# Casting one product's weights earlier in a convolution's out-projection, and two tiles that change places in the first feed-forward layer

## Chip, cores, metric

The kernel runs as one program on one core of a Trainium2 chip. The metric is device microseconds of an execution; less is better. The median of three runs before the change is 1311.68 us.

## The reference

The model is a trunk of two layers over 512 tokens of width 1024. Each layer has a token mixer and a SwiGLU feed-forward network, every sub-layer with normalisation before and after and with shift, scale and gate from a conditioning vector. Layer 0 mixes with a gated short convolution, layer 1 with a state-space scan. What matters here is the end of the first mixer and the start of the first feed-forward layer:

```python
def short_conv_mixer(h, w_in, conv_w, w_out):
    b_gate, c_gate, v = jnp.split(h @ w_in, 3, axis=-1)
    u = causal_depthwise_conv(c_gate * v, conv_w)
    return (b_gate * u) @ w_out
...
def swiglu_ffn(h, w_in, w_out):
    gate, up = jnp.split(h @ w_in, 2, axis=-1)
    return (jax.nn.silu(gate) * up) @ w_out
...
        y = short_conv_mixer(h, a_w_in[j], a_conv_w[j], a_w_out[j])
        x = x + gate * rmsnorm(y, norm_g[i, 1])
        h = rmsnorm(x, norm_g[i, 2]) * (1.0 + scale) + shift
        y = swiglu_ffn(h, f_w_in[i], f_w_out[i])
```

## The kernel before, in words

**Precision.** All large products are made of float32 values that are split in two: ScalarE casts the value to a rounded high part, VectorE subtracts the high part from the value to get the low part, and TensorE runs three matmuls (high by high, high by low, low by high). So each operand of TensorE has a cast on ACT and a subtraction on DVE behind it, and each weight tile (`whl`, a pool of four buffers) is free again when the last matmul that reads it is done.

**Order.** PE, ACT, DVE and SP each run their instructions in the order in which the source writes them; there is no planner in the two places that change. An instruction that waits holds up everything behind it on its engine.

**The out-projection of the convolution** (L1172 to L1288). Half of its inner dimension is computed with seven block products in place of eight. The table `PRODUCTS` names for each product the PSUM accumulator (A to D), the block of weights (`b11` to `b22`, or a sum that was made in place) and the block of activations. `product(i)` (L1137) is 12 matmuls of 128x512: two blocks of tokens, two blocks of the inner dimension, three parts each. `w_prep(i)` (L1120) casts the two weight blocks of product i on ACT (L1124) and subtracts on DVE (L1125). The products run in the order 1, 2, 0, 3, 4, 5, 6, with some plain matmuls (L408) between the later ones. Product 4 adds to accumulator A, which product 0 used before it, so A is first copied out to `part` (L1252, ACT). Ahead of product 3 the source has:

```python
            product(0)
            pa, pd, less = [tile4([P, 2, T], F32, "part") for _ in range(3)]
            for t in range(2):
                act.copy(pa[:, t, :], bank("A", t))
            lead, todo = ffn_lead(0, tile4), [[] for _ in range(5)]
            w_prep(4)
            product(3)
```

The `gate_b` of L1243 (L1095 on DVE, then the cast L1096 on ACT) makes the last block of gated activations; it stands between product 2 and product 0. The weights of product 4 are block `b22`, which is final once two accumulating DMAs of POOL (L610) have landed.

**The first feed-forward layer** starts while its first six column blocks are still being finished: `rest(i)` (L566) is 18 matmuls of 128x256 that complete block i, and they run in the order 0, 2, 1, 3, 4, 5. Their weights are the tiles `whl4`, which lie in a pool of 22 buffers of 4 KB per partition. Beside them DVE makes sums of the activations h: `vs.value(j)` (L742) adds the two parts of h again, j = 0 to 3 into the tile `va`, j = 4 to 7 into the tile `raw1`; `vs.sums`, `vs.hi` and `vs.lo` (L763, L764, L748, L753, L755) make the split sums `tq` out of them. SP fetches the first weights: `fetch(u)` (L627) loads two halves of a column block into `sg` (the tile `sums_w`, L632 and L633), adds them with an accumulating DMA of POOL (L640, shown in the profile as L1389) and loads another block into `wsu` (L635 to L638). Then come 12 units of seven products each (class `Units`, `product` with its matmuls on L693, 12 of 128x256). For the first unit the order on PE is P1, P5, P2, P6, P3, then P1 of the second unit, then P7 of the first. P6 and P7 use accumulator A again, and each waits until ACT has copied it out (`keep`, L703). On ACT the second `keep` of a unit stands behind the cast of the next unit's `sg` (`split_y`, L646), and that waits for DVE's `sum_y` (L672).

**Memory.** When the convolution's pool of 22 buffers is closed, the feed-forward layer's tiles are laid over the same bytes, in the order of their allocation. The first write into such a tile waits for the last access to each old buffer that lies under it, and for nothing else (`reuse_waits="tile"`). The second pool there is, in order: `tq1` (16 KB), `sums_w` (8 KB), `s1t`, `raw3`, `raw2`, `raw1`, `raw0` (8 KB each). `s1t` holds sums for the second half of the layer; its first write comes after the first units have begun.

Of the kernel before, what the change touches and what calls it, by code (L numbers as in the profile page):

```python
# [8 lines left out]
F32 = mybir.dt.float32  # L9
F32R = mybir.dt.float32r  # L10
# [6 lines left out]
P = 128  # L17
T = 512
# [13 lines left out]
MUL, ADD, SUB = ALU.mult, ALU.add, ALU.subtract  # L32
NS = 16
PRODUCTS = (("A", "b11", "a11"), ("B", "b21", "a12"), ("C", "b22", "a12"), ("D", "b12", "s1"),
            ("A", "b22", "a11"), ("A", "b11", "a21"), ("A", "b21", "a22"))
# [3 lines left out]
def trunk_kernel(  # L39
# [9 lines left out]
    act, dve, pe, pool = nc.scalar, nc.vector, nc.tensor, nc.gpsimd  # L49

    consts = ctx.enter_context(tc.tile_pool(name="consts", bufs=1))
    ps = ctx.enter_context(tc.tile_pool(name="ps", bufs=4, space=PSUM))
# [4 lines left out]
    whl_p = ctx.enter_context(tc.tile_pool(name="whl", bufs=4))  # L57
# [554 lines left out]
    class Units:  # L612
# [73 lines left out]
        def product(self, u, q):  # L686
            kind, k0, r = self.FACTORS[q]
            if q in self.FIRST:
                self.banks[r, u] = (aux_ps if r == "B" else mm_ps)(f"s{r}")
            dst, w = self.banks[r, u][:, HALVES[0]], self.wts[kind, u]  # L690
            for k in range(4):
                for i, (wl, al) in enumerate(((0, 0), (0, 1), (1, 0))):
                    pe.matmul(dst, w[:, wl, k0 + k, :], self.moving(q, k, al), skip_group_check=True,  # L693
                              start=q in self.FIRST and k == 0 and i == 0, stop=k == 3 and i == 2)
# [96 lines left out]
    with ExitStack() as ph:  # L791
# [14 lines left out]
        def tile4(shape, dtype, name):  # L806
            return actp.tile(shape, dtype, tag="a", name=name)
# [84 lines left out]
        def ffn_lead(i, tile4):  # L892
            w1 = f_w_in[i]
            return [lambda later=None, c0=c0: load_lead([(w1, c0, 256)], tile4, later) for c0 in (0, DFF, 256)]
# [7 lines left out]
        with tc.manual_schedule(engines={PE_ENGINE, mybir.EngineType.SP, mybir.EngineType.Activation,  # L902
# [183 lines left out]
            def gate_b(j, psb):  # L1086
                u = us[j]
                if j < 4:
                    if j % 2 == 0:
                        raw_c.append(tile4([P, 2, T], F32, "bur"))  # L1090
                    dve.tensor_mul(raw_c[j // 2][:, j % 2, :], psb, u)
                    acts.append(None)
                    return lambda: None
                a = act_tile(f"bu{j}")
                dve.tensor_mul(u, psb, u)  # L1095
                act.copy(a[:, 0, :], u)  # L1096
                acts.append(a)
                return lambda: dve.tensor_tensor(a[:, 1, :], u, a[:, 0, :].bitcast(F32), SUB)

            raw_c, rows_c, s1_c, w_c, a_c = [], [], [], {}, {}  # L1100
# [6 lines left out]
            def b_(name, p):  # L1107
                c = int(name[2]) - 1
                return rows_c[2 * p + int(name[1]) - 1][:, c * T:(c + 1) * T]

            def a_(name, p):
                if name == "s1":
                    return s1_c[0][:, p, :]
                return raw_c[p][:, int(name[2]) - 1, HALVES[int(name[1]) - 1]]

            def row_sums(dst, x, y, op):
                for p in range(2):
                    dve.tensor_tensor(a_(dst, p), a_(x, p), a_(y, p), op)

            def w_prep(i):  # L1120
                w = w_c[i] = whl_p.tile([P, 2, 2, T], F32R, tag="whl", name="whlo")
                for p in range(2):
                    src = b_(PRODUCTS[i][1], p)
                    act.copy(w[:, 0, p, :], src)  # L1124
                    dve.tensor_tensor(w[:, 1, p, :], src, w[:, 0, p, :].bitcast(F32), SUB)  # L1125
# [36 lines left out]
            def square_begin():  # L1162
                w_prep(2)
                for p in range(2):
                    add_(b_("b22", p), b_("b12", p))

            row45, st_c = [], []
            early = {7: begin_sums, 8: lambda: row_sums("a21", "a11", "a21", SUB), 9: lambda: a_prep(1),
                     10: lambda: a_prep(3), 11: lambda: a_prep(0), 12: sums_end, 13: lambda: a_prep(2),
                     14: lambda: (a_prep(4), a_prep(5)), 15: lambda: (w_prep(1), a_prep(6)), 16: lambda: (square_begin(), row_split()), 17: lambda: w_prep(0)}  # L1170

            for name in OPENING.split():  # L1172
# [18 lines left out]
            for k in range(18):  # L1191
                i, jp = k % 6, 2 + k // 6 * 2
# [42 lines left out]
            early[17]()  # L1235
            product(1)
            w_prep(3)
            product(2)
            row5, src5 = tile4([P, 2, T], F32R, "whl4"), st_c[0][:, 1, :]
            act.copy(row5[:, 0, :], src5)  # L1240
            next(fins[2])
            next(fins[2])
            lows.append(gate_b(KD - 1, tiles[17]))  # L1243
            dve.tensor_tensor(row5[:, 1, :], src5, row5[:, 0, :].bitcast(F32), SUB)
            row45.append((5, row5.rearrange("p i (k f) -> p i k f", k=1), 0))
            for p in range(2):
                add_(b_("b21", p), b_("b22", p))
# [3 lines left out]
            for t in range(2):  # L1251
                act.copy(pa[:, t, :], bank("A", t))  # L1252
            lead, todo = ffn_lead(0, tile4), [[] for _ in range(5)]
            w_prep(4)
            product(3)
            for t in range(2):
                act.copy(pd[:, t, :], bank("D", t))
# [37 lines left out]
        sa = st_p.enter_context(tc.tile_pool(name="sa", bufs=1, reuse_waits="tile"))  # L1295
# [2 lines left out]
        s_first.append(ffp.tile([P, 2, 4, P], F32R, tag="ffy", name="wss"))  # L1298
        tq.insert(0, sa.tile([P, 2, 2, 4, 256], F32R, tag="wxa", name="tq1"))
        sums_w = sa.tile([P, 2, 2, 4, P], F32, tag="wxb", name="sg")  # L1300
        s1t = sa.tile([P, NS // 2, 256], F32, tag="s1t", name="s1t")
        raw = [sa.tile([P, 4, T], F32, tag=f"raw{q}", name=f"raw{q}") for q in (3, 2, 1, 0)][::-1]
        wx, ff4 = [], []

        def s_tile(u):
# [189 lines left out]
        with tc.manual_schedule(engines={PE_ENGINE, mybir.EngineType.SP, mybir.EngineType.Activation,  # L1495
# [153 lines left out]
            for k in range(k0, last + 1):  # L1649
# [10 lines left out]
                q, j = divmod(k - 3, 4)  # L1660
# [42 lines left out]
            for q, item in enumerate(seq):  # L1703
                if item[0] == "s":
                    product(item)
                else:
                    w = w_of[item]
# [753 lines left out]
    with ExitStack() as ph:  # L2461
# [8 lines left out]
        raw = fb.tile([P, NF, T], F32, tag="raw", name="raw")  # L2470
# [418 lines left out]
```

## Time and profile before

| what | value |
|---|---|
| median of 3 runs | 1311.68 us (1311.48 to 1312.21) |
| the profiled execution's own time | 1312.8 us |
| its span, first to last instruction | 1311.0 us |
| PE, DVE, ACT, POOL busy | 99%, 80%, 56%, 10% of the span |
| mean granted TensorE clock | 0.999 |
| mean DMA traffic | 184 GB/s over the span |

In the timeline a row gives the start and the length in microseconds, the engine, the line and operation, what is written from what, how many instructions, and in brackets how long the engine had been idle and what ended that. PE is the matmuls, PEld the loading of their weights. In a windows row the last three numbers are the granted clock, the busy share of the DMA engines (over 1 where transfers queue) and GB/s.

### The profile page before, as it was taken

The page shows a single profiled execution, that of the slowest core. Times are in us where ns is not written, and L with a number is a line of the kernel's source. Part 1 is how long each engine was busy: PE and PEld are TensorE (multiplying, and loading weights), DVE is VectorE, ACT ScalarE, POOL GpSimd, SP SyncE. Part 2 cuts the span into 40 slices and gives each one's busy share as a digit, 9 for nine tenths or more (in the row PEclk, how much of TensorE's full clock was granted, in tenths as well). Part 3 has the DMA queues.
Part 4 walks back from the last instruction along what each step waited for, and adds up shares of the span by engine and source line. Part 5 has one row for each costly group of instructions (what it writes and reads, how often), then busy time and mean ns, then how long its engine had stood idle before and what let it go on. Part 6 is the DMA issues. An engine that isn't in the chain of part 4 may idle for free.

```text
span 1311.0 us, 20565 instructions
## 1 busy us (share of the span) xinstructions
PE 1296.9 (99%) x7841; PEld 1140.1 (87%) x7841; DVE 1045.0 (80%) x1598; ACT 735.0 (56%) x1301; POOL 126.7 (10%) x155
## 2 busy tenths in 40 slices
PE   8999999999999999999999999999999999999998
PEld 7788889899988888898888888888899999998886
DVE  5587998877866986769998999987878777766888
ACT  5423466455532565657765567755764555544665
POOL 0000011111100240000000000000100121101320
PEclk9999999999999999999999999999999999999999
DMA  9779661799868983437764457614432788878961
GB/s 307 230 257 297 183 192 50 193 234 239 204 193 272 257 161 106 156 105 232 230 215 152 141 184 217 184 50 150 156 97 63 193 219 205 203 195 288 177 123 64
DMA packets 225798, 241.69 MB, mean 184 GB/s; under 512 B 10516, under 2 KB 177316, under 8 KB 224676
## 3 DMA queue, kind: packets, MB, share of 16 engines
q1 hardware_dynamic: 203200, 193.00, 47.0%
q0 software_dynamic: 18496, 35.92, 15.2%
q10 hardware_dynamic: 4004, 11.46, 2.6%
q8 instruction: 61, 1.00, 0.3%
q14 instruction: 37, 0.30, 0.1%
HBM read 203.76 MB, written 4.34 MB: 159 GB/s over the span
## 4 chain that ended last, share of the span: by engine, by line
PE 88%; DVE 5%; ACT 2%; SPq 2%; DMA 2%; issue 1%; DVEq 0%; ACTq 0%
PE sA L693 12%; PE ip L305 10%; PE ip L307 9%; PE ip L306 9%; PE y L408 7%; PE sC L693 6%; PE cA L2596 5%; PE cA L1470 3%; PE sB L693 3%; PE li L305 2%; PE li L307 2%; PE li L306 2%; PE li L975 1%; PE y L2177 1%; PE yd L2005 1%
## 5 line engine op out<-in xcount | busy, mean ns | idle before, releaser
L305 PE MATMUL ip<-h,whl 128*128 128x512 f32 x640 | 252.6, 395 | 0.2 <-DVE cv L1075 0.2
L307 PE MATMUL ip<-h,whl 128*128 128x512 f32 x640 | 249.3, 390 | 0.0
L306 PE MATMUL ip<-h,whl 128*128 128x512 f32 x640 | 249.2, 389 | 0.0
L305 PEld LDWEIGHTS ip<-h,whl 128*128 128x128 f32 x640 | 120.2, 188 | 26.0 <-issue 1.8
L307 PEld LDWEIGHTS ip<-h,whl 128*128 128x128 f32 x640 | 120.1, 188 | 25.4
L306 PEld LDWEIGHTS ip<-h,whl 128*128 128x128 f32 x640 | 120.3, 188 | 24.0
L693 PE MATMUL sA<-tq,whl 128*128 128x256 f32 x1008 | 130.8, 283 | 1.4 <-ACT g L703 1.4
L693 PEld LDWEIGHTS sA<-tq,whl 128*128 128x128 f32 x1008 | 125.4, 192 | 2.1 <-ACT g L703 1.6
L232 DVE TENSOR_TENSOR whl<-wst,whl 128x1024 fp32r<-128x1024 f32 x70 | 85.2, 1220 | 22.2 <-ACT whl L231 22.2
L128 DVE SCALAR_TENSOR_TENSOR ada_acc<-ada_st,csil,ada_acc 128x1024 f32<-128x1024 f32 x70 | 89.7, 1281 | 3.8 <-DMA ada_st<-in_ada_w_dram 2.6
L305 PE MATMUL li<-h,whl 128*128 128x256 f32 x288 | 83.5, 290 | 0.0
L307 PE MATMUL li<-h,whl 128*128 128x256 f32 x288 | 81.6, 283 | 0.0
L306 PE MATMUL li<-h,whl 128*128 128x256 f32 x288 | 81.5, 283 | 0.0
L231 ACT CAST whl<-wst 128x1024 fp32r<-128x1024 f32 x70 | 72.6, 1040 | 7.3 <-DMA wst<-in_a_w_in_dram 4.5
L408 PE MATMUL y<-whlo,ys 128*128 128x512 f32 x288 | 67.3, 391 | 0.0
L1857 DVE SCALAR_TENSOR_TENSOR cu<-ip,cols,cu 128x511 f32<-128x511 f32 (+2 forms) x84 | 62.7, 746 | 3.4 <-ACT cu L1854 1.4
L408 PEld LDWEIGHTS y<-whlo,ys 128*128 128x128 f32 x288 | 53.8, 188 | 11.5 <-issue 0.4
L2596 PE MATMUL cA<-whlo,ao 128*128 128x512 f32 x264 | 61.0, 390 | 0.4 <-DVE c L2802 0.2
L2596 PEld LDWEIGHTS cA<-whlo,ao 128*128 128x128 f32 x264 | 49.3, 188 | 11.5 <-ACT whlo L2561 1.2
L305 PEld LDWEIGHTS li<-h,whl 128*128 128x128 f32 x288 | 55.2, 192 | 0.8 <-issue 0.8
L306 PEld LDWEIGHTS li<-h,whl 128*128 128x128 f32 x288 | 55.2, 192 | 0.0
L307 PEld LDWEIGHTS li<-h,whl 128*128 128x128 f32 x288 | 55.1, 191 | 0.0
(453 smaller groups left out, 2738.6 us busy)
## 6 DMA issues: line engine op xcount, KB each, us to landing
ada_st<-in_ada_w_dram SPq DMA_DIRECT2D x96, 512.0 KB, 6.5
wsu<-in_f_w_in_dram SPq DMA_DIRECT2D x30, 512.0 KB, 5.2
sg<-in_f_w_in_dram SPq DMA_DIRECT2D x56, 256.0 KB, 3.5
wsu<-in_f_w_in_dram SPq DMA_DIRECT2D x56, 256.0 KB, 4.8
wst<-in_m_w_in_dram SPq DMA_DIRECT2D x14, 1024.0 KB, 6.0
wst<-in_f_w_in_dram SPq DMA_DIRECT2D x10, 1024.0 KB, 5.2
wst<-in_m_w_in_dram SPq DMA_DIRECT2D x20, 512.0 KB, 4.7
wst<-in_a_w_in_dram SPq DMA_DIRECT2D x9, 1024.0 KB, 7.4
```

Of the source, the lines that this page charges most:

```text
L128: dve.scalar_tensor_tensor(acc, w, csil[:, k:k + 1], acc, MUL, ADD)
L231: later.append((lambda sw=sw, w=w: act.copy(w[:, 0, :nk, :], sw), lambda sw=sw, w=w: dve.tensor_tensor(w[:, 1, :nk, :], sw, w[:, 0, :nk, : ...
L232: lambda sw=sw, w=w: dve.tensor_tensor(w[:, 1, :nk, :], sw, w[:, 0, :nk, :].bitcast(F32), SUB)))
L305: pe.matmul(dst, w_at(w, 0, kk), a[:, 0, sl], start=start, stop=False)
L306: pe.matmul(dst, w_at(w, 0, kk), a[:, 1, sl], start=False, stop=False)
L307: pe.matmul(dst, w_at(w, 1, kk), a[:, 0, sl], start=False, stop=stop)
L408: pe.matmul(pst, a[:, al, tk], wt[:, wl, kk, :], start=i == 0 and k == (opens[hf][t] if opens else 0), stop=k == K - 1 and i == 2, skip_gr ...
L693: pe.matmul(dst, w[:, wl, k0 + k, :], self.moving(q, k, al), skip_group_check=True, start=q in self.FIRST and k == 0 and i == 0, stop=k == ...
L975: pe.matmul(acc_of(i), w[:, part // 2, k, c0:c0 + P], h[kk][:, part % 2, :], start=(kk, part) == (0, 0), stop=(kk, part) == (KD - 1, 2))
L1470: pe.matmul(bank[r, sub], a[:, al, q, tk], w[:, wl, q, :], start=first and k == 0, stop=False, skip_group_check=True)
L1857: dve.scalar_tensor_tensor(u[:, sft:], pst[:, :T - sft], w[3 - sft], u[:, sft:], MUL, ADD)
L2596: pe.matmul(bank[r][sub], a[:, al, q, tk], w[:, hl, q, :], start=first and k == 0, stop=last and k == 2, skip_group_check=True)
```

## The change

**First part.** The preparation of product 4's weights is taken from its place behind the copies of accumulator A and cut in two: the casts (`w_cast(4)`) go ahead of the gating on ACT, behind the cast of `row5`; the subtractions (`w_low(4)`) go behind `row5`'s subtraction on DVE. Nothing is added or removed.

**Second part.** `raw1` and `s1t` change places in the pool: `raw1` is allocated first and `s1t` last but one. All tiles are of the same size, so each takes the other's bytes.

```diff
+            def w_cast(i):
+                w_c[i] = whl_p.tile([P, 2, 2, T], F32R, tag="whl", name="whlo")
+                for p in range(2):
+                    act.copy(w_c[i][:, 0, p, :], b_(PRODUCTS[i][1], p))
+
+            def w_low(i, ps=(0, 1)):
+                w = w_c[i]
+                for p in ps:
+                    dve.tensor_tensor(w[:, 1, p, :], b_(PRODUCTS[i][1], p), w[:, 0, p, :].bitcast(F32), SUB)
...
             act.copy(row5[:, 0, :], src5)
+            w_cast(4)
             next(fins[2])
             next(fins[2])
             lows.append(gate_b(KD - 1, tiles[17]))
             dve.tensor_tensor(row5[:, 1, :], src5, row5[:, 0, :].bitcast(F32), SUB)
+            w_low(4)
...
             lead, todo = ffn_lead(0, tile4), [[] for _ in range(5)]
-            w_prep(4)
             product(3)
...
         sums_w = sa.tile([P, 2, 2, 4, P], F32, tag="wxb", name="sg")
+        raw1 = sa.tile([P, 4, T], F32, tag="raw1", name="raw1")
+        raw3, raw2 = [sa.tile([P, 4, T], F32, tag=f"raw{q}", name=f"raw{q}") for q in (3, 2)]
         s1t = sa.tile([P, NS // 2, 256], F32, tag="s1t", name="s1t")
-        raw = [sa.tile([P, 4, T], F32, tag=f"raw{q}", name=f"raw{q}") for q in (3, 2, 1, 0)][::-1]
+        raw = [sa.tile([P, 4, T], F32, tag="raw0", name="raw0"), raw1, raw2, raw3]
```

On ACT, between the cast of `row5` (`whl_1535`) and the copies of accumulator D, before the change (`whlo` from `wrow` are product 4's weights, `bu` the gated activations, `part` the copies of A and then of D):

```order
L1240 CAST whl_1535<-wsto 128x512 [waits Pool_49]
L1096 CAST bu_1544<-u_cv 128x512 [waits DVE_49]
L1252 COPY part<-y_1552 128x512 [waits PE_49]
L1252 COPY part<-y_1553 128x512 [waits PE_49]
L1124 CAST whlo<-wrow 128x512 [waits DMASW2_49,Activation_49]
L1124 CAST whlo<-wrow 128x512 [waits DMASW3_49]
L1257 COPY part<-y_1576 128x512 [waits PE_49]
```

The same place on ACT after the change:

```order
L1250 CAST whl_1535<-wsto 128x512 [waits Pool_49]
L1123 CAST whlo<-wrow 128x512 [waits DMASW2_49,PE_49,Activation_49]
L1123 CAST whlo<-wrow 128x512 [waits DMASW3_49]
L1096 CAST bu_1547<-u_cv 128x512 [waits DVE_49]
L1264 COPY part<-y_1557 128x512 [waits PE_49]
L1264 COPY part<-y_1558 128x512 [waits PE_49]
L1268 COPY part<-y_1576 128x512 [waits PE_49]
```

The two casts moved past three instructions of ACT. The wait on PE that they now name is for the last matmul of product 1, whose weight buffer they take. On DVE the two subtractions keep their place between `row5`'s subtraction and the addition of `part` to accumulator B; they stand there before and after, but depend on casts that come earlier.

On DVE, where the sums of h begin, before the change (the number behind a name counts tiles in the order of their allocation):

```order
L128 SCALAR_TENSOR_TENSOR ada_acc_116<-ada_st_2242,csil_94,ada_acc_116 128x1024 [waits DMAHW6_49]
L128 SCALAR_TENSOR_TENSOR ada_acc_116<-ada_st_2244,csil_94,ada_acc_116 128x1024 [waits DMAHW7_49,DVE_49]
L742 TENSOR_TENSOR raw1_2237<-h4_1745 128x512 [waits PE_49]
L742 TENSOR_TENSOR raw1_2237<-h5_1746 128x512
L753 TENSOR_TENSOR tq1_2232<-va_2241,tq1_2232 128x1024 [waits Activation_49]
```

The same place on DVE after the change:

```order
L128 SCALAR_TENSOR_TENSOR ada_acc_116<-ada_st_2242,csil_94,ada_acc_116 128x1024 [waits DMAHW6_49]
L128 SCALAR_TENSOR_TENSOR ada_acc_116<-ada_st_2244,csil_94,ada_acc_116 128x1024 [waits DMAHW7_49,DVE_49]
L742 TENSOR_TENSOR raw1_2234<-h4_1745 128x512 [waits PE_49]
L742 TENSOR_TENSOR raw1_2234<-h5_1746 128x512
L753 TENSOR_TENSOR tq1_2232<-va_2241,tq1_2232 128x1024 [waits Activation_49]
```

No instruction moved here. What the first L742 waits for on PE is another matmul. Traced back through the values of the semaphores, the built programs differ in these waits beside those of the moved casts:

- The first write into `raw1` (L742, DVE) waited for the last matmul of `rest(3)`, whose weights lay under `raw1`. Now it waits for the last matmul of `rest(1)`, whose weights lay under `s1t` and now lie under `raw1`.
- The first load into `sg` (L632, SP) and its accumulating DMA (L1389, POOL) waited for the sixth of the 18 matmuls of `rest(3)`. Now they wait for the last matmul of `rest(2)`. This comes from the first part: with the casts in another order, the pool's buffers come free in another order, and two `whl4` tiles (a half of the weights of `rest(2)` and a half of those of `rest(3)`) take each other's buffers.
- Near the end of the layer one cast of the next stage's weights (L213, ACT) waits for a subtraction that reads `s1t` (L214) in place of one that reads `raw1`; four other instructions gain or lose a wait for something that ended long before.

## The prediction

> **What bounds the kernel now.** I read the page first: the busy shares, and the chain of work that ended last by engine.
>
> ```profile
> PE 1296.9 (99%) x7841; PEld 1140.1 (87%) x7841; DVE 1045.0 (80%) x1598; ACT 735.0 (56%) x1301; POOL 126.7 (10%) x155
> PE 88%; DVE 5%; ACT 2%; SPq 2%; DMA 2%; issue 1%; DVEq 0%; ACTq 0%
> ```
>
> TensorE is busy for 1296.9 of 1311.0 us. The change adds and removes no matmul, so it can only win or lose at places where PE stands still. I therefore asked next for the waits of PE and of its weight loads, from 186 to 520 us, and for those of the weight loads from 165 to 200 us.
>
> ```profile
> PE sA L693 <- ACT g L703: 1.4, 1, 1.4
> PEld sA L693 <- ACT g L703: 1.6, 1, 1.6
> PEld y L1146 <- DVE whlo L1125: 0.5, 1, 0.5
> PEld y L1146 <- ACT whlo L1124: 0.3, 1, 0.3
> ```
>
> One wait lies at each of the two places that change: L1146 is the out-projection, L693 the feed-forward units. How long they are on PE's path I took from the timeline, since a wait's row also counts time in which the loads run ahead.
>
> **First part: the casts for product 4.** The timeline of PE, and of ACT, DVE and POOL beside it:
>
> ```profile
> 168.21 3.91 PE L1146 MATMUL y<-whlo,ao 128*128 128x512 f32 x16
> 172.34 2.79 PE L1146 MATMUL y<-whlo,ao 128*128 128x512 f32 x11 [0.22 <-DVE whlo L1125]
> 174.97 1.52 PE L408 MATMUL y<-whl,bu 128*128 128x512 f32 x6
> 176.33 2.88 PE L1146 MATMUL y<-whlo,ao 128*128 128x512 f32 x12
> 179.05 1.52 PE L408 MATMUL y<-whl,bu 128*128 128x512 f32 x6
> ...
> 164.09 0.62 ACT L1240 CAST whl<-wsto 128x512 fp32r<-128x512 f32 x1
> 169.46 0.62 ACT L1096 CAST bu<-u_cv 128x512 fp32r<-128x512 f32 x1 [4.75 <-DVE u_cv L1095]
> 169.98 1.06 ACT L1252 COPY part<-y 128x512 f32<-128x512 f32 x2
> 170.94 1.15 ACT L1124 CAST whlo<-wrow 128x512 fp32r<-128x512 f32 x2
> ...
> 169.34 0.68 DVE L1244 TENSOR_TENSOR whl<-wsto,whl 128x512 fp32r<-128x512 f32 x1
> 171.60 1.29 DVE L1125 TENSOR_TENSOR whlo<-wrow,whlo 128x512 fp32r<-128x512 f32 x2 [1.58 <-ACT whlo L1124]
> ...
> 164.50 2.85 POOL L1248 TENSOR_TENSOR wrow<-wrow 128x512 f32<-128x512 f32 x2
> ```
>
> Undisturbed, 12 matmuls take 179.05 - 176.33 = 2.72 us, 0.227 each. From 168.21 to 174.97 there are 16 + 11 = 27, which is 6.12 us; they took 6.76. **The stall is 0.64 us.** ACT was idle for 4.75 us before 169.46, waiting for the gating, with product 4's casts queued behind. Now they start behind the cast of L1240, at 164.71, and end near 165.9. They also wait for product 1, two products ahead of product 0, and for `b22`, which has landed: POOL's L1248 reads it at 164.50. The subtractions start when DVE is through with L1244, at about 170.0, and the two end at 171.3 (1.29 us).
>
> Product 4's first matmul is due at 168.21 + 15 x 0.227 = 171.6. The copies of A end at 169.98 + 1.06 = 171.04, in time by 0.6 us; the first subtraction ends near 170.7, before the second matmul (171.8), the other before the fifth. Nothing takes the stall's place. Next late could be product 5: it is due at 171.6 + 2.72 + 1.36 (six plain matmuls) = 175.7. Its casts come on ACT behind the copies of D, which can end 0.6 us after product 3 does at 171.8, at 172.4, and take 1.15, like those of product 4; its subtractions are done 0.7 later, near 174.3. Gain: 0.64 us. If DVE or ACT were busy where I take them to be free, the bound is zero gain.
>
> A rule speaks against it. Of the 14 subtractions of this kind one took 3447 ns where the median is 684, and POOL's L1248 is the only work of POOL beside them that reads SBUF:
>
> ```profile
> L1125 DVE TENSOR_TENSOR whlo<-wrow,whlo x14: 680/684/3447, 151.2 to 177.0; 128x512 fp32r<-128x512 f32 x14
> ```
>
> The Trainium skill (SBUF — State Buffer, "Who interferes with whom") says that a VectorE instruction with two SBUF inputs and a GpSimd instruction that reads SBUF shut each other out of a shared port for the whole instruction; the row agrees. Here the moved subtractions start 2.6 us after POOL's L1248 ended at 167.35. Were they to meet it, the first would end at 170.0 + 3.45 = 173.4, PE would stand for 173.4 - 171.8 = 1.6 us, and the sum below would lose those 1.6 us (1310.8 us). Since nothing moves them that far ahead, I give it 0.01.
>
> **Second part: where the sums of h may start.** PE's products of the first units, and what ACT, DVE, SP and POOL do before:
>
> ```profile
> 251.13 1.59 PE L693 MATMUL sA<-h,whl 128*128 128x256 f32 x12
> 252.56 1.60 PE L693 MATMUL sC<-tq,whl 128*128 128x256 f32 x12
> 254.00 1.60 PE L693 MATMUL sB<-h,whl 128*128 128x256 f32 x12
> 261.53 1.69 PE L693 MATMUL sA<-tq,whl 128*128 128x256 f32 x12 [1.42 <-ACT g L703]
> 263.06 1.60 PE L693 MATMUL sC<-tq,whl 128*128 128x256 f32 x12
> ...
> 233.95 0.60 ACT L1339 ACTIVATE g<-li 128x512 f32<-128x512 f32 x1 [1.08 <-PE li L307]
> 260.16 1.04 ACT L646 CAST whl<-sg 128x1024 fp32r<-128x1024 f32 x1 [3.16 <-PE sA L693]
> 261.11 0.36 ACT L703 COPY g<-sA 128x256 f32<-128x256 f32 x1
> ...
> 233.00 1.28 DVE L128 SCALAR_TENSOR_TENSOR ada_acc<-ada_st,csil,ada_acc 128x1024 f32<-128x1024 f32 x1
> 236.11 1.30 DVE L742 TENSOR_TENSOR raw<-h 128x512 f32<-128x512 f32 x2 [1.82 <-PE li L307]
> 244.53 1.23 DVE L753 TENSOR_TENSOR tq<-va,tq 128x1024 fp32r<-128x1024 f32 x1 [0.74 <-ACT tq L748]
> 246.80 0.68 DVE L672 TENSOR_TENSOR sg<-sg,wsu 128x512 f32<-128x512 f32 x1
> 259.33 0.68 DVE L672 TENSOR_TENSOR sg<-sg,wsu 128x512 f32<-128x512 f32 x1
> ...
> 234.66 0.38 SPq L632 DMA_DIRECT2D sg<-in_f_w_in_dram  x1
> 239.60 0.87 POOL L1389 DMA_DIRECT2D sg<-sg  x1 [11.44 <-DMA sg<-in_f_w_in_dram]
> sg<-sg POOLq DMA_DIRECT2D x1, 256.0 KB, 6.9
> 233.00:235.00 2.00, 2.00 (x19) 2.00 (x18) 1.28 (x1) 0.60 (x1) 0.00 (x0) 1.00 0.00 0
> 239.00:241.00 2.00, 2.00 (x16) 1.87 (x15) 1.97 (x5) 0.00 (x0) 0.87 (x1) 1.00 1.02 305
> ```
>
> A product undisturbed takes 254.00 - 252.56 = 1.44 us. From 251.13 to 263.06 there are seven, 10.08 us; they took 11.93. **The stall is 1.85 us**, nearly all at P7 (261.53). P7 waits for the copy L703 at 261.11, and that for the cast L646 at 260.16. The row puts this cast down to PE, but the product whose buffer it takes had ended by 255.6; what it needs last is the sum L672, which ends on DVE at 260.01. DVE's chain there goes back, over short idle times like that ahead of L753, to L742 at 236.11, which sat 1.82 us behind `rest(3)`.
>
> Now L742 waits for the end of `rest(1)`. The activation L1339 of ACT waits for the same matmul and starts at 233.95, so at 234.28, when L128 ends, nothing holds L742: it starts **1.82 us earlier**, and what follows it on DVE too, as long as nothing else holds it. P7 is due at 251.13 + 6 x 1.44 = 259.77; the copy would let it start at 261.53 - 1.82 = 259.71. That just covers the stall.
>
> The one thing that would hold it is the first `sg` sum: L672 at 246.80 needs POOL's accumulating DMA, issued at 239.60 and landed 6.9 us later, at 246.5. If that stayed, L672 could only move by 0.3 us, and so would P7: the second part alone is worth about 0.3. But the loads of `sg` now wait for the end of `rest(2)`. That is 6 matmuls of `rest(3)` and 18 of `rest(1)` earlier, 24 of 0.12 us (1.44 / 12), 2.9 us: SP issues at 231.8 into DMA engines that stood idle (share 0.00 from 233 to 235). The accumulation then lands near 243.6, and L672 is free for its new time, 246.80 - 1.82 = 244.98. So both parts are needed for the 1.85. Weights, further `sg` loads and additions follow in the same order, each 1.8 to 2.9 us earlier.
>
> Between the two readings, 0.3 us and 1.85 us, I take **1.8**, since the cover is 1.82 for a stall of 1.85. The moved wait of L213 costs nothing: the cast waits in any case behind another on ACT, by which time the subtraction is done.
>
> **The sum.** 0.64 + 1.8 = 2.44 us. From 263 us to the end PE is the chain, apart from two short stretches, and the loads there are issued as earlier work frees buffers, so I let the gain reach the end. The profiled execution would take 1312.8 - 2.4 = 1310.4 us; the median of the runs stands 1.1 us below that execution (1311.68), so the forecast is 1311.68 - 2.44 = **1309.2 us**. A difference of 0.2%, 2.6 us, is about what a measurement of this kernel can tell from no change; the forecast is just inside that.
>
> **Rivals.**
>
> *Only part of it arrives.* The DMA engines are saturated from 239 us on (share 1.02), and if the accumulation lands late or DVE loses some of its lead, the second part is worth between 0.3 and 1.5: 1309.5 to 1310.7 us. For it: P7's cover is 0.06 us. Against: each step's lead, 1.8 us, is that of a whole chain. Chance 0.15.
>
> *The gain is given back later.* At 449 us PE waits again, for DVE behind a transfer; if that transfer is paced by DMA traffic alone, up to the whole 2.4 is lost there: 1310.5 to 1311.7. For it:
>
> ```profile
> 431.60 1.28 DVE L128 SCALAR_TENSOR_TENSOR ada_acc<-ada_st,csil,ada_acc 128x1024 f32<-128x1024 f32 x1 [0.79 <-DMA ada_st<-in_ada_w_dram]
> 449.35 2.15 PEld L1470 LDWEIGHTS cA<-whlo,ao 128*128 128x128 f32 x10 [0.90 <-DVE ao L1451]
> ```
>
> Against: SP issues that transfer only when DVE has used a buffer, which follows PE. Chance 0.08. Were the wait of 0.9 to shrink as well, the time would be 1309.2 - 0.9 = 1308.3 us: chance 0.08.
>
> *Slower: the loads collide.* The weights and `ada_st` now come while the first `sg` is still being added. The Trainium skill (DMA: Bandwidth & Descriptors, "Issuing engines are not separate DMA queues") says that transfers of all issuers share the same 16 engines and interleave; no run here shows the two apart. In rows: the accumulation, issued at about 236.7, took 6.9 us in traffic of share 1.02. From 8.3 us on (landing at 245.0) it holds L672 back, and each further microsecond costs PE one. To end slower by 2.6 us than before it has to lose 2.44 + 2.6 = 5.0, so it would have to take over 13 us; that gives 1314.3. Chance 0.04.
>
> **How the numbers follow.** The forecast's case has 0.64, the lock 0.01. The three runs shown lie 0.7 us apart and the terms are known to some 0.3, so 0.23 of the 0.64 falls beyond 2.6 us; with the 0.08 of the shrinking wait faster has 0.31. Slower has 0.04, the rest, 0.65, is within 0.2%. The range runs from 1308.5, both stalls gone and that spread on top, to 1311.2, which takes in the partial case, the lock and half of the later loss.
>
> **What would show it.** Right: no wait of L1146 for product 4's weights; L742 on `raw1` without idle time before it; the first L632 about 2.9 us earlier against PE, and P7 without a wait; span near 1311.0 - 2.4 = 1308.6 us. Wrong: a wait of L672 for the `sg` addition, P7 still waiting for L703, or PE's wait at 449 grown by what was won.

## The result, and the profile after

The changed kernel takes 1309.67 us (median of 11 runs, 1308.98 to 1310.51). The kernel before takes 1312.21 us in the same series (11 runs, 1311.48 to 1314.29). The medians differ by 2.5 us. The ratio is estimated at 0.9979 (that of the medians is 0.9981), 95% interval 0.9969 to 0.9988: about 0.2% less, and the interval leaves out no change. The profiled execution of after took 1308.98 us, its span is 1307.2.

Busy times of after, and the chain of work that ended last:

```profile
PE 1295.1 (99%) x7841; PEld 1139.7 (87%) x7841; DVE 1045.2 (80%) x1598; ACT 735.2 (56%) x1301; POOL 126.7 (10%) x155
PE 95%; SPq 2%; ACT 1%; DMA 1%; DVE 1%; issue 0%; DVEq 0%
```

PE's share of the chain rose from 88% to 95%, and DVE's fell from 5% to 1%. The chain goes over to DVE where PE waited for it and then follows DVE's own work, so these shares say that PE waited less for DVE, but not how much was won: 4% of the span would be 52 us, the gain is 2.5. In the changed file the lines from 1119 on have moved: the matmuls L1146 of the out-projection are now L1156, the subtraction for product 4 is L1128, its casts L1123, POOL's accumulations L1402, and the third place's matmuls L1483 (L1470 before).

The timeline of after at the first place (PE, ACT, DVE):

```profile
160.26 5.60 PE L1156 MATMUL y<-whlo,ao 128*128 128x512 f32 x24
165.85 8.44 PE L1156 MATMUL y<-whlo,ao 128*128 128x512 f32 x36
174.12 1.52 PE L408 MATMUL y<-whl,bu 128*128 128x512 f32 x6
164.41 1.14 ACT L1123 CAST whlo<-wrow 128x512 fp32r<-128x512 f32 x2
169.74 1.29 DVE L1128 TENSOR_TENSOR whlo<-wrow,whlo 128x512 fp32r<-128x512 f32 x2
```

The 36 matmuls of products 0, 3 and 4 are one row without a wait. The two subtractions take 1.29 us together, so nothing shut them out.

At the second place (SP, POOL, DVE, ACT, PE):

```profile
230.93 0.38 SPq L632 DMA_DIRECT2D sg<-in_f_w_in_dram  x1
235.35 0.87 POOL L1402 DMA_DIRECT2D sg<-sg  x1 [8.04 <-PE li L307]
233.36 1.29 DVE L742 TENSOR_TENSOR raw<-h 128x512 f32<-128x512 f32 x2
244.05 0.68 DVE L672 TENSOR_TENSOR sg<-sg,wsu 128x512 f32<-128x512 f32 x1
258.37 0.36 ACT L703 COPY g<-sA 128x256 f32<-128x256 f32 x1
250.28 1.60 PE L693 MATMUL sA<-h,whl 128*128 128x256 f32 x12
258.91 1.60 PE L693 MATMUL sA<-tq,whl 128*128 128x256 f32 x12
260.35 1.60 PE L693 MATMUL sC<-tq,whl 128*128 128x256 f32 x12
```

L742 on `raw` and L672 start without idle time, the copy L703 ends at 258.73, and P7 starts at 258.91 without a wait. From 250.28 to 260.35 are 10.07 us, where before it was 11.93.

The two spans differ by 3.8 us, the medians by 2.5. Most of that 1.3 us lies at a third place, near 449 us before, where PE needs the activations of the fourth product (L1451 on DVE, L1464 after). In the profiled execution of before PE waited there; in that of after it did not:

```profile
437.25 10.76 PEld L1483 LDWEIGHTS cA<-whlo,ao 128*128 128x128 f32 x48
```

That row is 48 weight loads without a break. Whether this belongs to the change is one question of the experiments.

### The profile page after: what moved, and what is told of

The parts are those of the page before. It is cut to its first block, busy times and chain, and to the rows that moved or that the text cites. A ratio compares the mean times of both kernels' runs of the same rounds, so it can differ in the third digit from the quotient of the medians.

```text
span 1307.2 us, 20564 instructions
## 1 busy us (share of the span) xinstructions
PE 1295.1 (99%) x7841; PEld 1139.7 (87%) x7841; DVE 1045.2 (80%) x1598; ACT 735.2 (56%) x1301; POOL 126.7 (10%) x155
## 4 chain that ended last, share of the span: by engine, by line
PE 95%; SPq 2%; ACT 1%; DMA 1%; DVE 1%; issue 0%; DVEq 0%
PE sA L693 12%; PE ip L305 11%; PE ip L307 11%; PE ip L306 11%; PE y L408 7%; PE sC L693 6%; PE cA L2609 5%; PE cA L1483 3%; PE sB L693 3%; PE li L305 3%; PE li L307 3%; PE li L306 3%; PE li L975 2%; PE y L1156 1%; PE y L2190 1%; PE yd L2018 1%
## 5 line engine op out<-in xcount | busy, mean ns | idle before, releaser
L408 PE MATMUL y<-whlo,ys 128*128 128x512 f32 x288 | 67.3, 391 | 0.0
L408 PEld LDWEIGHTS y<-whlo,ys 128*128 128x128 f32 x288 | 53.8, 188 | 11.5 <-issue 0.4
```

What stands on the lines that cost most here:

```text
L408: pe.matmul(pst, a[:, al, tk], wt[:, wl, kk, :], start=i == 0 and k == (opens[hf][t] if opens else 0), stop=k == K - 1 and i == 2, skip_gr ...
```

## The experiments

Besides the prediction's theory (two stalls, the second needing an early L742 and an early `sg`), three rivals were open: L742 alone is enough; the early `sg` alone is enough; part of the gain is the wait at the third place. All kernels below were profiled; the second look at before has a single time, the others ten or eleven. From each timeline I read four stretches of PE, each between rows that start the same instruction in every kernel, and give what they exceed the undisturbed length by: from the first `x24` row of the out-projection to L408 (undisturbed 13.85 us), from P1 to the product behind P7 (10.07), from there to the matmul L148 (176.56), and from L148 to the first weights of the next accumulator cB (11.13).

| kernel | median us | ratio to before (95%) | product 4 | P6, P7 | later units | third place | span |
|---|---|---|---|---|---|---|---|
| before | 1312.21 | | 0.65 | 1.86 | 0.00 | 0.79 | 1311.0 |
| before, again (e8) | one run | | 0.64 | 1.86 | 0.01 | 0.00 | 1310.3 |
| both parts | 1309.67 | 0.9969 to 0.9988 | 0.01 | 0.00 | 0.00 | 0.01 | 1307.2 |
| both, again (e4) | 1309.93 | 0.9973 to 0.9991 | 0.00 | 0.00 | 0.01 | 0.87 | 1308.1 |
| first part only (e1) | 1312.81 | 0.9992 to 1.0010 | 0.00 | 2.06 | 0.79 | 1.27 | 1311.5 |
| second part only (e2) | 1311.96 | 0.9990 to 1.0008 | 0.63 | 1.48 | 0.00 | 1.70 | 1310.7 |
| both, sg late (e3) | 1313.45 | 0.9999 to 1.0017 | 0.00 | 3.76 | 0.00 | 1.63 | 1313.1 |
| second part, sg early (e5) | 1312.07 | 0.9989 to 1.0007 | 0.63 | 0.09 | 1.78 | 0.24 | 1310.3 |
| third place eased only (e6) | 1311.99 | 0.9987 to 1.0005 | 0.64 | 1.86 | 0.01 | 0.08 | 1310.6 |
| both, third place eased (e7) | 1309.21 | 0.9966 to 0.9985 | 0.00 | 0.00 | 0.00 | 0.01 | 1307.1 |
| both, sg earlier still (e9) | 1310.73 | 0.9979 to 0.9997 | 0.00 | 0.10 | 1.64 | 1.36 | 1310.5 |
| first part, order kept (e10) | 1312.15 | 0.9989 to 1.0006 | 0.01 | 1.86 | 0.00 | 0.34 | 1309.8 |
| second part, sg early, order kept (e11) | 1310.75 | 0.9979 to 0.9997 | 0.67 | 0.00 | 0.00 | 1.09 | 1309.0 |
| the same, third place eased (e12) | 1309.92 | 0.9974 to 0.9991 | 0.62 | 0.00 | 0.01 | 0.00 | 1308.4 |

The stretches of a row are those of one execution. Less its four excesses, every span is 1306.9 to 1308.0 us. So these four stretches hold nearly all that sets the kernels apart; what is left is mostly the opening of the kernel, which differs by up to 0.8 us (the first row of the out-projection starts between 159.87 and 160.67), and a wait of 0.56 us in e6 and of 0.28 in e12 further on. Before had a median of 1312.47, 1312.2 and 1312.51 us in the three series with the experiments (33, 26 and 33 runs).

**e1, the first part alone.** The kernel before with only this of the diff:

```diff
             act.copy(row5[:, 0, :], src5)
+            w_cast(4)
...
             dve.tensor_tensor(row5[:, 1, :], src5, row5[:, 0, :].bitcast(F32), SUB)
+            w_low(4)
...
-            w_prep(4)
```

> Only the earlier casts and subtractions of product 4's weights; raw1 and s1t stay where they were. In this build the first sg load waits for the end of rest(2), as with both parts, and L742 for the end of rest(3), as before. Theory (each part has its stall, and P7 needs an early L742 and an early sg): the out-projection's stall of 0.64 us is gone, P7's of 1.85 us stays, since the chain from L742 is as late as before: 0.6 us under the kernel before. Rival (the late sg load alone set P7): P7's stall goes here too, and the kernel is 2.4 us faster. Rival for the third place (PE's wait of 0.9 us at 449 us, for DVE): if the casts' part is what removed it, 1.5 us faster.

Measured: 1312.81 us, no faster than before. The stall at product 4 is gone as expected and P7's stays, so the rival that the early `sg` alone is enough is refuted, and so is the one that the casts removed the wait at the third place (1.27 us here). But 0.2 us were added to P7's stall and 0.8 behind it. The timeline of this kernel (PE, ACT, POOL, SP):

```profile
260.82 1.70 PE L693 MATMUL sA<-tq,whl 128*128 128x256 f32 x12 [1.60 <-ACT g L703]
265.67 0.50 PE L693 MATMUL sA<-tq,whl 128*128 128x256 f32 x2 [0.27 <-DVE g L720]
262.98 1.05 ACT L655 CAST whl<-wsu 128x1024 fp32r<-128x1024 f32 x1 [1.69 <-DMA wsu<-in_f_w_in_dram]
244.09 0.88 POOL L1400 DMA_DIRECT2D sg<-sg  x1 [7.96 <-DMA sg<-in_f_w_in_dram]
250.08 0.87 POOL L1400 DMA_DIRECT2D wsu<-wsu  x1 [5.12 <-DVE raw L1368]
244.88 0.37 SPq L635 DMA_DIRECT2D wsu<-in_f_w_in_dram  x1
```

And the same of after:

```profile
243.94 0.88 POOL L1402 DMA_DIRECT2D sg<-sg  x1 [7.72 <-DMA sg<-in_f_w_in_dram]
246.75 0.87 POOL L1402 DMA_DIRECT2D wsu<-wsu  x1 [1.94 <-DMA wsu<-in_f_w_in_dram]
243.03 0.37 SPq L635 DMA_DIRECT2D wsu<-in_f_w_in_dram  x1
```

In e1 POOL issues the accumulation of the second `sg` (244.09) ahead of SP's loads into the second `wsu` (244.88); the accumulation into `wsu`, which needs those loads, follows 5.2 us behind them. In after the loads (243.03) go 0.9 us ahead of the accumulation, and it is 3.7 us. The DMA issues of the two kernels, with the time from issue to landing at the end of a row, e1 first and after second:

```profile
wsu<-in_f_w_in_dram SPq DMA_DIRECT2D x2, 256.0 KB, 4.6
wsu<-in_f_w_in_dram SPq DMA_DIRECT2D x2, 256.0 KB, 3.1
```

The early `sg` came from the buffers, but `wsu` waits for DVE, whose chain behind L742 was still late. So the order of the two transfers turned round. That is a new theory: an accumulation that gets ahead of the loads makes them 1.5 us slower, and the units behind P7 pay for it. (The 4.6 and 3.1 us are medians of two loads in one execution each.)

**e2, the second part alone.** The kernel before with `raw1` and `s1t` exchanged:

```diff
+        raw1 = sa.tile([P, 4, T], F32, tag="raw1", name="raw1")
+        raw3, raw2 = [sa.tile([P, 4, T], F32, tag=f"raw{q}", name=f"raw{q}") for q in (3, 2)]
         s1t = sa.tile([P, NS // 2, 256], F32, tag="s1t", name="s1t")
-        raw = [sa.tile([P, 4, T], F32, tag=f"raw{q}", name=f"raw{q}") for q in (3, 2, 1, 0)][::-1]
+        raw = [sa.tile([P, 4, T], F32, tag="raw0", name="raw0"), raw1, raw2, raw3]
```

> Only raw1 and s1t change places; product 4's weights are prepared where they were. L742 waits for the end of rest(1); the first sg load still waits for the sixth matmul of rest(3). Theory: L742 starts 1.8 us earlier against PE, but the sum L672 waits for the sg accumulation, so P7's stall falls only from 1.85 to about 1.5 us, the L1146 stall of 0.64 stays: 0.3 us under the kernel before. Rival (the chain from L742 is all that counts, the sg accumulation has room): P7's stall goes, 1.85 us faster.

Measured: 1311.96 us; the interval takes in 0.3 us less as well as no change, and excludes 1.85 less. The timeline shows why (DVE, PE):

```profile
233.64 1.28 DVE L742 TENSOR_TENSOR raw<-h 128x512 f32<-128x512 f32 x2
245.83 0.69 DVE L672 TENSOR_TENSOR sg<-sg,wsu 128x512 f32<-128x512 f32 x1 [1.41 <-DMA sg<-sg]
260.57 1.70 PE L693 MATMUL sA<-tq,whl 128*128 128x256 f32 x12 [1.22 <-ACT g L703]
```

L742 is early and without idle time, but L672 stands 1.41 us behind the accumulation of `sg`, and P7 still waits. The excess fell by 0.38. The rival that L742 alone is enough is refuted.

**e3, both parts with a late sg.** The changed kernel, with `sums_w` and `s1t` exchanged in the pool:

```diff
+        s1t = sa.tile([P, NS // 2, 256], F32, tag="s1t", name="s1t")
-        sums_w = sa.tile([P, 2, 2, 4, P], F32, tag="wxb", name="sg")
         raw1 = sa.tile([P, 4, T], F32, tag="raw1", name="raw1")
         raw3, raw2 = [sa.tile([P, 4, T], F32, tag=f"raw{q}", name=f"raw{q}") for q in (3, 2)]
-        s1t = sa.tile([P, NS // 2, 256], F32, tag="s1t", name="s1t")
+        sums_w = sa.tile([P, 2, 2, 4, P], F32, tag="wxb", name="sg")
```

> Both parts, and sg changes places with s1t, so that its first load waits for the end of rest(3): 18 + 18 matmuls of 0.12 us later than with both parts (4.3 us), 1.4 later than before. Theory: L672 waits for the accumulation until about 1.1 us later than it started before; P7 stands still for 1.85 + 1.1 = 2.9 us; 2.9 us slower than both parts, 0.5 us slower than before. Rival (the sg accumulation has room): no stall at P7, the time of both parts.

Measured: 1313.45 us, 3.5 over both parts in the same series. L672 and the two products that wait:

```profile
248.18 0.69 DVE L672 TENSOR_TENSOR sg<-sg,wsu 128x512 f32<-128x512 f32 x1 [3.01 <-DMA sg<-sg]
256.93 1.70 PE L693 MATMUL sA<-tq,whl 128*128 128x256 f32 x12 [1.82 <-ACT g L703]
262.92 1.70 PE L693 MATMUL sA<-tq,whl 128*128 128x256 f32 x12 [1.42 <-ACT g L703]
```

The direction is the theory's, the size was not: 3.76 us of stall, where 2.9 were expected, because P6 now waits as well as P7, for the copy of the same accumulator. Together with e2 this shows that an early `sg` is needed.

**e4, both parts again.** No edit.

> The changed kernel once more, in the same series. Theory: about 2.5 us under the kernel before; no stall at product 4 and at P7. At the third place, the fourth of the products of the layer's second matrix (449 us before), PE needed its activations 0.02 us after they were ready in the profiled execution, so in another execution a wait of 0 to 0.5 us. Rival (the two stalls are not all that systematically differs: the wait of 0.9 us goes in every execution): 3.4 us under the kernel before.

Measured: 1309.93 us, 2.5 under before. Both stalls are gone again, to 0.01 us, but this execution did wait at the third place:

```profile
446.55 2.14 PEld L1483 LDWEIGHTS cA<-whlo,ao 128*128 128x128 f32 x10 [0.99 <-DVE ao L1464]
```

So the missing wait in the first profile of after was not the change's doing. The rival, that it goes in every execution, is refuted.

**e8, the kernel before again.** No edit.

> The kernel before once more, for a second look at what repeats. Theory: stalls of 0.64 us at product 4 and of 1.85 us at P7 to within 0.1; the wait at the third place another than 0.9 us, between 0.5 and 2. Rival (all three are fixed): 0.9 us again.

Measured: 1312.08 us. The two stalls repeat to 0.01 us; the third wait is absent, where the first profile of before had 0.9:

```profile
440.14 10.76 PEld L1470 LDWEIGHTS cA<-whlo,ao 128*128 128x128 f32 x48
```

It is absent in one execution and there in another of the same kernel, so the theory was right that it varies, and too narrow (0.5 to 2). What goes with it is the time from a load, SP's `wst`, to the cast that needs it. Both are shown for the first profile of before, for e8 and for e2:

```profile
415.62 0.43 SPq L1646 DMA_DIRECT2D wst<-in_f_w_in_dram  x1
423.06 1.05 ACT L1642 CAST whl<-wst 128x1024 fp32r<-128x1024 f32 x1 [2.95 <-DMA w2x<-in_f_w_out_dram]
415.78 0.43 SPq L1646 DMA_DIRECT2D wst<-in_f_w_in_dram  x1
422.45 1.05 ACT L1642 CAST whl<-wst 128x1024 fp32r<-128x1024 f32 x1 [2.50 <-DMA w2x<-in_f_w_out_dram]
414.95 0.43 SPq L1648 DMA_DIRECT2D wst<-in_f_w_in_dram  x1
422.88 1.05 ACT L1644 CAST whl<-wst 128x1024 fp32r<-128x1024 f32 x1 [3.50 <-DMA wst<-in_f_w_in_dram]
```

The first two rows put the cast's wait down to `w2x`, a load issued 0.5 us behind `wst`, so which of the two loads is late is not shown there. From the issue of `wst` to the cast it takes 7.4, 6.7 and 7.9 us, and the excess at the third place is 0.79, 0.00 and 1.70. Of the eleven executions in which this place was not eased, the four with up to 6.9 us have an excess of 0.00 to 0.34, the seven with 7.4 to 7.9 have 0.79 to 1.70. That the loads' time causes the wait is argued from this and from DVE's chain behind it; no run set that time by hand.

**e5, the second part with an early sg.** The kernel before; the first part is left out, and `sums_w` changes places with `raw3`, so that its first load waits for the sixth matmul of `rest(2)`:

```diff
-        sums_w = sa.tile([P, 2, 2, 4, P], F32, tag="wxb", name="sg")
-        s1t = sa.tile([P, NS // 2, 256], F32, tag="s1t", name="s1t")
-        raw = [sa.tile([P, 4, T], F32, tag=f"raw{q}", name=f"raw{q}") for q in (3, 2, 1, 0)][::-1]
+        raw3 = sa.tile([P, 4, T], F32, tag="raw3", name="raw3")
+        raw1 = sa.tile([P, 4, T], F32, tag="raw1", name="raw1")
+        sums_w = sa.tile([P, 2, 2, 4, P], F32, tag="wxb", name="sg")
+        raw2 = sa.tile([P, 4, T], F32, tag="raw2", name="raw2")
+        s1t = sa.tile([P, NS // 2, 256], F32, tag="s1t", name="s1t")
+        raw = [sa.tile([P, 4, T], F32, tag="raw0", name="raw0"), raw1, raw2, raw3]
```

> The casts stay late (no first part); raw1 and s1t change places, and sg and raw3 too, so that the first sg load waits for a matmul of rest(2). Theory (P7 needs an early L742 and an early sg; the first part gives the second only through the buffers): P7's stall of 1.85 us goes, the 0.64 at product 4 stays: 1.9 us under the kernel before, 0.6 over both parts. Rival (an early sg helps only with product 4's casts early as well): P7's stall stays above 1 us.

Measured: 1312.07 us (1310.16 to 1315.31), not 1.9 under before. P7's stall did go, without the first part, so the rival is refuted. But 1.78 us came back behind it. The timeline (PE, POOL, SP) and the waits of PE:

```profile
264.45 3.14 PE L693 MATMUL sA<-tq,whl 128*128 128x256 f32 x24 [0.31 <-DVE g L720]
PE sA L693 <- DVE raw L720: 1.0, 1, 1.0
243.15 0.88 POOL L1392 DMA_DIRECT2D sg<-sg  x1 [7.38 <-DMA sg<-in_f_w_in_dram]
243.69 0.37 SPq L635 DMA_DIRECT2D wsu<-in_f_w_in_dram  x1
```

It is the same reversal as in e1: the accumulation goes 0.5 us ahead of the loads. Three runs test this.

**e9, both parts with sg earlier still.** The changed kernel with the pool's order of e5: `sg` 1.4 us earlier, everything else as in after.

> Both parts, and sg changes places with raw3, so that its first load waits for the sixth matmul of rest(2), 1.4 us earlier than with both parts. Theory of the order of two transfers (where POOL's accumulation of the second sg is issued ahead of SP's loads of the second wsu, these take about 4.7 us instead of 3.1, and the weights behind them come late): the accumulation now goes ahead of the loads by some 0.5 us, the wsu accumulation comes 5.2 us behind the loads instead of 3.7, and PE waits for L720 after P7: 0.5 to 1.8 us slower than both parts, with runs spread over more than 2 us. Rival (an earlier sg can't hurt): the time of both parts.

Measured: 1310.73 us (1309.31 to 1312.97), 0.8 over the 1309.93 of both parts in their own series; the two intervals against before overlap. The profiled execution took 1312.31 us, so it is one of the longer runs of this kernel. In it POOL, then SP, then POOL, and PE:

```profile
242.06 0.88 POOL L1403 DMA_DIRECT2D sg<-sg  x1 [7.44 <-DMA sg<-in_f_w_in_dram]
242.73 0.37 SPq L635 DMA_DIRECT2D wsu<-in_f_w_in_dram  x1
247.98 0.87 POOL L1403 DMA_DIRECT2D wsu<-wsu  x1 [5.05 <-DVE raw L1371]
263.55 3.14 PE L693 MATMUL sA<-tq,whl 128*128 128x256 f32 x24 [0.36 <-DVE g L720]
```

The order is reversed by 0.7 us, `wsu`'s accumulation follows the loads by 5.2 us, and 1.64 us come back in the later units. The runs spread over 3.7 us, against 1.5 in e4: four of the eleven lie above 1312 us, where no run of e4 is above 1310.72. So earlier is not better here.

**e10, the first part with the order kept.** e1, and for the second fetch POOL's two accumulations exchanged, so that the one into `sg` can't go ahead of the loads:

```diff
-            if u < self.count:
+            if u < self.count and u != 1:
                 add_(flat2(sg[:, 0]), flat2(sg[:, 1]))
             if u:
                 add_(flat2(st[:, 8:12, :]), flat2(self.staged[u - 1][0][:, 0:4, :]))
+            if u == 1:
+                add_(flat2(sg[:, 0]), flat2(sg[:, 1]))
```

> First part alone, and in the second fetch POOL issues the accumulation into wsu ahead of that into sg, so that the latter can't run ahead of SP's loads of wsu. Theory of the order: loads of wsu take 3.1 us again, the wait for L720 goes, P7's stall is 1.85 us as before, and the first part's 0.64 us arrives: 0.6 under the kernel before, 0.6 to 1 under the first part alone. Rival (the first part is worth nothing for another reason): the time of before.

Measured: 1312.15 us, 0.4 under before in its series, but the interval takes in no change. By the stretches it is the theory's: 0.01 at product 4, 1.86 at P7, nothing later. The third place had 0.34 in this execution. By the time alone the rival is not excluded.

**e11, the second part with an early sg and the order kept.** e5 with the edit of e10.

> Second part with an early sg, without the first part, and the same order of POOL's accumulations. Theory of the order: P7's stall goes and no wait for L720 takes its place; only the 0.64 us at product 4 is left of the two: 1.8 us under the kernel before, 0.6 over both parts. Rival (the wait for L720 comes from the late casts of product 4): 0.3 us under before, as without the new order.

Measured: 1310.75 us, 1.8 under before (0.9979 to 0.9997). The accumulations in POOL and the loads of SP, and P7:

```profile
243.31 0.37 SPq L635 DMA_DIRECT2D wsu<-in_f_w_in_dram  x1
247.12 0.88 POOL L1394 DMA_DIRECT2D wsu<-wsu  x1 [11.46 <-DMA wsu<-in_f_w_in_dram]
259.19 1.60 PE L695 MATMUL sA<-tq,whl 128*128 128x256 f32 x12
```

3.8 us from the loads to the accumulation, P7 without a wait, and 0.00 in the later units, where e5 had 1.78. Only the order of two accumulations differs, so the order alone took e5's gain; e1 and e10 are a second such pair (0.79 and 0.00). This rests on the stretches: the profiled executions of e5 and e11 each have their kernel's median time, but the two medians come from different series and their intervals overlap.

**e6 and e7, the third place eased.** In the kernel before (e6) and in the changed kernel (e7), the first three preparations of activations go ahead of those of weights:

```diff
+                if q < 3:
+                    a_prep(seq[q + 3])
                 if q + 4 < len(seq):
                     w_prep(seq[q + 4])
-                if q + 3 < len(seq):
+                if 3 <= q < len(seq) - 3:
                     a_prep(seq[q + 3])
```

> Kernel before, with the preparation of the activations for the products 3 to 5 of the layer's second matrix ahead of the weights for the products 4 to 6: 1.2 us of DVE no longer lie ahead of the values that PE waits for at the third place. Theory (that wait is there in nearly every execution, 0.9 to 1.9 us, and is on the path): 0.9 to 1.5 us under the kernel before, and its runs lie closer together than the 2.3 us of before. Rival (DVE is late there as a whole, so the next product waits instead): within 0.5 us of before.

> Both parts with the same reordering at the third place. Theory: the wait of 0 to 1 us there goes, so 0.5 to 1 us under both parts, near 1309.0, and its runs lie within 1 us. Rival: the time of both parts, 1309.9, since another wait takes its place.

Measured: e6 1311.99 us, no difference from before that the runs can tell. The wait shrank to 0.19 us and another came three products later (weight loads of PE in e6, and in e7):

```profile
448.45 2.15 PEld L1470 LDWEIGHTS cA<-whlo,ao 128*128 128x128 f32 x10 [0.19 <-DVE ao L1451]
457.05 4.86 PEld L1470 LDWEIGHTS cB<-whlo,ao 128*128 128x128 f32 x22 [0.56 <-DVE ao L1451]
436.97 10.76 PEld L1483 LDWEIGHTS cA<-whlo,ao 128*128 128x128 f32 x48
```

So for e6 the rival was right. e7 has the lowest median of all, 1309.21 us, and 10 runs within 1.0 us (1308.84 to 1309.87). It is 0.5 to 0.7 us under both parts in the two series that measured them, but the intervals against before overlap. The spread is smaller (1.0 us against 1.5 in both), the gain of the median is not settled.

**e12, all eased but without the first part.** e11 with the edit of e7.

> As the run before it, and with the activations ahead of the weights at the third place. It differs from the kernel with both parts and the third place eased in the first part alone (and in where sg lies and the order of two accumulations). Theory: the 0.64 us of the first part, so 0.6 us slower than that one, near 1309.9. Rival (where nothing else stands in the way, the stall at product 4 is made up later): the same time, 1309.2.

Measured: 1309.92 us, 0.7 over e7 (0.4 when each is taken against before in its own series); the only excess among the four stretches is the 0.62 us at product 4. The two kernels were timed in different series, and their intervals overlap, so the first part's price rests on the stretches, which agree in all fourteen executions (0.62 to 0.67 without it, 0.00 to 0.01 with it), more than on the medians.

## Why the prediction was right

**The sum.** It held: 0.64 + 1.8 = 2.44 us were forecast, the two stretches give 0.64 + 1.86 = 2.50, the medians 2.54. The forecast of 1309.2 us is 0.5 below the 1309.67 measured, and this is because the median of before that it starts from, 1311.68 of three runs, lay 0.5 below that of the eleven.

**Product 4.** Each step stands. The casts run at 164.41 (164.71 forecast, in an execution that is 0.2 us earlier at this place), the subtractions at 169.74 (170.0), nothing takes the stall's place, and product 5 is not late. The port lock that the Trainium skill describes (SBUF — State Buffer, "Who interferes with whom") did not strike: the two took 1.29 us.

**P7.** L742 moved by 1.9 us against PE (1.82 forecast): 236.11 - 233.36 less the 0.85 by which PE was earlier there. The load of `sg` moved by 2.9 us (2.9). "Both parts are needed" was right: with the second alone, P7's stall fell by 0.38 (0.3 forecast), and e3 and e2 show L672 behind the accumulation. e5 and e11 show that P7 needs the first part only for what it does to the buffers.

**The third place.** Two rivals spoke of it. Neither "given back later" nor "shrinks as well" is what happens: the wait differs between executions of one kernel, 0.79 and 0.00 us before, 0.01 and 0.87 after. The two profiles that were compared first happened to show its two ends, hence a difference of the spans of 3.8 us, and a span of 1307.2 where 1308.6 was forecast. The four-stretch sum for these is 0.64 + 1.86 + 0.78 = 3.3; 0.2 lies in the opening; the last 0.3 I did not place.

**What the prediction missed** is the form of the collision. It priced an accumulation, that of the first `sg`, that lands late, beyond 8.3 us; in after it took 7.2. It did not see that an accumulation can be the one that harms: in e1, e5 and e9 that of the second `sg` took no more than 4.6 us and made the loads issued behind it late, which cost PE up to 1.8 us. The prediction took it that further loads and additions follow "in the same order". With both parts they do, by a margin of 0.7 to 0.9 us (243.03 against 243.94 in the first profile of after), because both `sg` and, through L742, `wsu` come forward. That margin was in none of its terms, so it is luck in this respect that nothing behind P7 took the gain back. The first part alone has no such margin: for it the sum has 0.64 us, and it brought nothing that could be measured. The Trainium skill (DMA: Bandwidth & Descriptors, "Issuing engines are not separate DMA queues") says that DMAs of all issuers run on the same 16 engines and interleave. The traces agree in part. In e1, from 241.0 to 241.5 us, 43 packets of POOL's queue and 45 of SP's ran side by side. But from 245.5 to 248.0 all 128 packets, 0.26 MB, were the accumulation's, and the loads issued at 244.88 and 245.29 moved none, where in after the first packets of these loads moved 1.0 to 1.5 us behind the issue. There the two did not interleave, and the order of issue decided which of them paid.

## What to carry to other kernels

When a tile's first write waits for another tile's last read, a change in the order of two casts can move a load by microseconds far away: trace the waits through the buffers, not through the lines of the diff. A transfer that starts earlier is a gain only as long as it doesn't get ahead of one that is needed sooner; look at the order of issue on both sides of the change, and fix that order where the margin is under a microsecond. And before a difference between two profiles is put down to a change, profile the same kernel a second time: here a wait of 0.8 us came and went by itself.

## What the runs showed of the hardware

The two loads of 256 KB into the second `wsu` took 2.9 to 3.2 us where they were issued ahead of the accumulating DMA of 256 KB into the second `sg` (before, e8, after, e4, e6, e7 and e10 to e12), and 4.6 to 4.7 where they were issued 0.5 to 0.8 us behind it (e1, e5, e9). In e2 and e3 they were issued ahead of it too and yet took 4.1 and 6.1 us: there the accumulation into the first `sg` was still on its way, until 245.9 and 248.1, when they were issued at 243.31 and 243.38. Both would fit a rule that any accumulation under way slows a load, but other loads were on their way there too, and no run takes the two apart. The accumulation took 4.4 to 4.6 us where it was first, and 6.4 to 7.2 where it was issued 0.7 to 0.9 us behind the loads (after, e4, e7). While the accumulation goes, the DMA engines are busy but move little. The windows of e1 and then of after (the last three numbers are clock, DMA share, GB/s):

```profile
245.00:247.00 2.00, 2.00 (x10) 1.67 (x9) 2.00 (x3) 0.40 (x2) 0.00 (x0) 1.00 0.79 85
245.00:247.00 2.00, 2.00 (x10) 1.65 (x10) 1.48 (x3) 0.82 (x1) 0.25 (x1) 1.00 1.05 273
```

A share of 0.79 with 85 GB/s stands against 1.05 with 273. In the window of e1 all 83 packets are of POOL's queue, in that of after all 1083 are of SP's, though in both kernels the accumulation and the loads had been issued by 245.3 us. And in two executions of the same kernel one 512 KB load took 6.7 and 7.4 us from its issue to its first use, with nothing changed; the profile puts the end of both waits down to a load issued right behind it.
